# The weights of one stretch split into high and low parts by DMAs instead of by two engines

## The chip, the cores and the metric

The kernel runs on one core of one Trainium2 chip. The metric is the device time of one execution in microseconds. Engine names are those of the profile: PE is the matrix engine (PEld its weight loads), DVE the vector engine, ACT the scalar engine, POOL the general engine, SP the engine that issues most DMAs. Before the change two runs took 1109.42 and 1110.84 us, median 1110.13 us.

## What is computed

One decoder layer over 512 tokens of 2048 features, in float32: an input RMSNorm, one projection with 7728 columns, attention in three branches (NSA, 16 heads), a gated linear recurrence (HGRN2, 8 heads), a norm and a SiLU gate on each group's output, an output projection, the residual and a last norm. Cut to what matters here:

```
h = rmsnorm(x, norm_in[l])
proj = h @ w_in[l]
(q_a, k_cmp, v_cmp, k_slc, v_slc, k_win, v_win, gate_a, z_a,
 q_h, f_h, i_h, z_h) = jnp.split(proj, split_at, axis=-1)
o_a = nsa_mixer(q_a, k_cmp, ...)
o_h = hgrn2_mixer(q_h, f_h, i_h, lbs[l])
o_a = head_rmsnorm(o_a, nsa_out_norm[l], NSA_HEADS) * jax.nn.silu(z_a)
o_h = head_rmsnorm(o_h, hgrn_out_norm[l], HGRN_HEADS) * jax.nn.silu(z_h)
x = x + jnp.concatenate([o_a, o_h], axis=-1) @ w_out[l]
return rmsnorm(x, final_norm)
```

The products of the projections need more precision than one pass of PE's rounded type (float32r) gives. So each operand is written as a sum of a rounded high part and a float32r low part, and each product takes three matmuls: high by high, high by low, low by high.

## The kernel before, in words

**A load.** The weights come in pieces of 512 KB, 1024 columns of 128 partitions (two tiles of 512 columns in `proj_tm`, lines 342 to 344, four tiles of 256 in `proj_fm`, lines 317 to 319). `load_w` (line 269) makes one piece ready: `load_raw` issues its DMA on SP (line 139), ACT rounds it into the high part (the CAST of line 275), DVE subtracts that from the raw piece into the low part (line 276). Then PE runs 24 matmuls of 512 columns on the piece. Raw, high and low each take one of ten buffers of the pool `w` (`WBUF`), so one piece holds three of them until PE, or for the raw one DVE, is done.

**The stretch of the change** begins with `hgrn_v(0)` (the values of four HGRN2 heads) and ends where the output projection begins. It has 72 pieces: 8 of `hgrn_v(0)`; then 44 while the eight heads of `hgrn_head` run between them; then 20 for the gates (`z_proj`) with `gate_chunk` between them. A head is a chain of small steps: DVE scales its keys and queries level by level, POOL copies one piece of queries (line 737), ACT copies others (lines 747, 751, 771, 792, 802, 814), and PE makes the products from them (lines 722, 767, 778, 800, 810, 812).

**What sets the order.** `run` draws pieces of several generators in the ratio of their stated costs. A scheduler then places each engine's instructions; from there each engine goes through its own list strictly in order, and an instruction that waits holds everything behind it on that engine. DMAs are issued in the same way by the engine in whose list they stand.

Of the kernel before, what the change touches and what calls it, by code (L numbers as in the profile page):

```python
# [10 lines left out]
FP32 = mybir.dt.float32  # L11
F32R = mybir.dt.float32r
I32 = mybir.dt.int32
AF = mybir.ActivationFunctionType
ALU = mybir.AluOpType
AX = mybir.AxisListType

P = 128
# [25 lines left out]
def hymba_layer(ctx: ExitStack, tc: tile.TileContext, x, norm_in, w_in, pe_k, w1_k, w2_k,  # L44
# [43 lines left out]
    def run(*gens):  # L88
        """Emits the pieces of several streams, each at the pace of its stated cost."""
        st = [[g, t, 0.0] for g, t in gens]  # L90
        while st:
            e = min(st, key=lambda e: e[2] / e[1])
            try:
                c = next(e[0])
                e[2] = max([o[2] / o[1] for o in st if o is not e]) * e[1] + 1e-6 if c is None else e[2] + c
            except StopIteration:
                st.remove(e)

    def chain(*gens):
        for g in gens:  # L100
            yield from g

    def upto(gen, cost):
        """The stream's next pieces, up to a cost."""
        while cost > 0:
            c = next(gen, None)
            if c is None:
                return
            cost -= c
            yield c  # L110
# [18 lines left out]

# [1 line left out]
    warm = const.tile([1, 1], FP32, name="warm")  # L131
# [9 lines left out]

    # the input by columns: first features and number of tiles of each step, its tiles of tokens, its weights
    FIRST = ((0, 2), (2, 2), (4, 4), (8, 4), (12, 4))
# [24 lines left out]

# [1 line left out]
    hT = [[], []]  # L170
# [29 lines left out]
    def x_norm():  # L200
        """The factor of each token: on the partitions, its half, and along the columns."""
        ss = sm(NT, "ss")
        nc.vector.tensor_reduce(ss, ss_in, AX.X, ALU.add)
        nc.vector.tensor_copy(rs[:, 0, :], rsqrt(ss, NT, 1.0 / D, "rx"))
        nc.vector.tensor_scalar(rs[:, 1, :], rs[:, 0, :], 0.5, None, ALU.mult)
        bp = ps_tp()
        for t in range(NT):
            nc.tensor.transpose(bp[:, t * P:(t + 1) * P], rs[:, 0, t:t + 1].broadcast_to([P, P]), ident)
        nc.scalar.copy(rs_bc, bp)
# [19 lines left out]

# [1 line left out]
    dist = const.tile([P, 512], FP32, name="dist")  # L231
# [27 lines left out]

    # rows that a block of right-hand columns takes, for each level: first row and width within the step  # L260
    for mi, (h, step, lo, width) in enumerate([(1, 2, 0, 1), (2, 4, 0, 2), (4, 8, 2, 2), (4, 8, 0, 2),
# [5 lines left out]

# [1 line left out]
    def load_w(src, k0, kt, c0, c, wt=None, raw=None):  # L269
        if raw is None:  # L270
            raw = load_raw(src, k0, kt, c0, c)
        if wt is None:
            wt = (b4("w", WBUF, F32R), b4("w", WBUF, F32R))
        hi, lo = [w[:, 0:kt * c].rearrange("p (k c) -> p k c", k=kt) for w in wt]
        nc.scalar.copy(hi, raw)  # L275
        nc.vector.tensor_tensor(lo, raw, hi.bitcast(FP32), ALU.subtract)  # L276
        return hi, lo
# [26 lines left out]
    def proj_fm(acc, c0, c):  # L304
        """Columns c0.. of the projection, features on the partitions; accumulators are appended to acc."""
        n = c // P
        kt = min(8, WCOLS // c)
        acc += [pj() for _ in range(n)]
        mm = 0.215 * 3
        for k0 in range(0, NK, kt):  # L310
            hi, lo = load_w(w_in2, k0, kt, c0, c)
            for j in range(n):
                for k in range(kt):
                    kk = k0 + k
                    hh, hl = hT[0][kk], hT[1][kk]
                    wh, wl = hi[:, k, j * P:(j + 1) * P], lo[:, k, j * P:(j + 1) * P]
                    nc.tensor.matmul(acc[j], wh, hh, start=kk == 0, stop=False)  # L317
                    nc.tensor.matmul(acc[j], wh, hl, start=False, stop=False)  # L318
                    nc.tensor.matmul(acc[j], wl, hh, start=False, stop=kk == NK - 1)  # L319
                    if k % 4 == 3 or k == kt - 1:  # L320
                        yield mm * (k % 4 + 1)

    def proj_tm(acc, src, aT, c0, c, done=None):
        """The same with tokens on the partitions: aT is stationary, the weights move."""
        kt = WCOLS // c
        acc += [pj() for _ in range(NT)]
        mm = 0.215 * 3 * c / 512
        groups = [[(k0, min(kt, NK - k0))] for k0 in range(0, NK, kt)]
        if len(groups) > 2:
            groups[-2:] = [groups[-2] + groups[-1]]  # L330
        for gr in groups:
            end = sum(gr[-1])
            while end > len(aT[0]):
                yield None
            ws = [load_w(src, k0, n, c0, c) for k0, n in gr]
            for t in range(NT):
                o = acc[t][:, 0:c]
                for (k0, n), (hi, lo) in zip(gr, ws):
                    for k in range(n):
                        kk = k0 + k  # L340
                        ah, al = aT[0][kk][:, t * P:(t + 1) * P], aT[1][kk][:, t * P:(t + 1) * P]
                        nc.tensor.matmul(o, ah, hi[:, k, :], start=kk == 0, stop=False)  # L342
                        nc.tensor.matmul(o, al, hi[:, k, :], start=False, stop=False)  # L343
                        nc.tensor.matmul(o, ah, lo[:, k, :], start=False, stop=kk == NK - 1)  # L344
                if done is not None and end == NK:
                    done(t, acc[t])
                yield mm * (end - gr[0][0])

# [1 line left out]
    kc_hi = const.tile([P, P], F32R, name="kc_hi")  # L350
# [5 lines left out]
    def blocks(acc, pcol):  # L356
        """Shifted copies of the projected rows, then the blocks with their position terms."""
        kv = []
# [75 lines left out]

# [1 line left out]
    def split_dma(acc_ps, scale, dsts):  # L436
# [12 lines left out]
    def make_kd(g2, b):  # L449
        """Keys of a branch for two groups: the parts hi and lo, each on both halves of the partitions.  # L450
        The keys of the second branch have the compressed ones in front."""
        acc = []
# [52 lines left out]
    def scores(e, i, b):  # L505
        """Scores of a tile of queries and what the softmax makes of them; the sum comes along."""
        h, yv = e["h"], e["yv"]
# [25 lines left out]
    def flip(e, i, b, y):  # L533
        """The weights with the keys on the partitions."""
        n = (i + 1) * P
# [24 lines left out]
    def weigh(e, i):  # L560
        """Values times weights for two tiles of queries, the two branches on two halves of the array."""
        g = e["h"] // 4
# [105 lines left out]

# [1 line left out]
    o_h = [None] * HH  # L670

    def hgrn_head(hh, x0, f, vt):
# [43 lines left out]
        def mm192(x, sections):  # L716
            """Products of the 128 keys of each tile with 192 columns; the masked parts go to dg."""
            for jp in range(2):
# [15 lines left out]

        # the diagonal and level 1
        for jp in range(2):
# [49 lines left out]
        off = lv["off"]  # L786
        # keys with the tokens on the partitions, states at the ends of the tiles
        tps = ps_tp()
# [57 lines left out]

# [1 line left out]
    mT = [[], []]  # L848
# [50 lines left out]

# [1 line left out]
    KC, VC = [], []  # L901
# [10 lines left out]
    fill = [make_q(1), make_q(2), make_kd(1, 0), make_q(3), make_kd(1, 1)] + [make_q(p) for p in range(4, 8)]  # L912
    run((attention(), 160), (chain(*fill, hgrn_qf(0)), 135))
    run((hgrn_v(0), 41))
    sz = [[] for _ in range(4)]
# [7 lines left out]

# [1 line left out]
    ys = [[None] * 4 for _ in range(NT)]  # L925
# [25 lines left out]
    def last_chunk():  # L951
        for t in range(NT):
# [16 lines left out]
            nc.vector.tensor_scalar(pre, pre, 1.0 / D, EPS, ALU.mult, ALU.add)  # L969
            # 1 / sqrt of the mean square: a guess from the bits, then three steps of Newton  # L970
            v, g, u = [a[:, i:i + 1] for i in range(3)]
# [7 lines left out]
            for c in (1, 0, 2, 3):  # L979
# [7 lines left out]
                nc.sync.dma_start(out=out2[t * P:(t + 1) * P, c * 512:(c + 1) * 512], in_=y)  # L987

    last_w = []
    for c in range(3):  # L990
# [39 lines left out]
```

## Time and profile before

| | |
|---|---|
| median of the runs | 1110.13 us |
| span of the profiled execution | 1109.5 us |
| PE busy | 1090.7 us (98%) |
| DVE busy | 579.9 us (52%) |
| ACT busy | 395.7 us (36%) |
| POOL busy | 71.3 us (6%) |
| DMA queue of SP | 108.65 MB, 34.1% of 16 engines |

A span runs from the first to the last instruction of one profiled execution. Busy is the time in which an engine has an instruction in work. Consecutive matmuls overlap, so a busy PE is judged by the start of each matmul against the start of the next. "Idle before" an instruction is put down to what ended it.

### The profile page before, as it was taken

To read this page: it belongs to the slowest core of one execution; us is meant where nothing else is said; L and a number is where in the kernel's file an instruction comes from. 1 tells how busy PE (TensorE), PEld (TensorE's weight loads), DVE (VectorE), ACT (ScalarE), POOL (GpSimd) and SP (SyncE) were. 2 spreads that over 40 slices of the span, in tenths; PEclk is the share of its full clock that TensorE was granted. 3 is DMA by queue.
4 is the path that set the end of the run, shared out by engine and by line. 5 is a ranking of instruction groups with operands and counts; after the bars stand their busy time and mean duration, and the time that the engine had idled before them with its cause. 6 is when DMAs were issued, how large, how long until landed. Compare 5 with 4: busy or idle time off the path is not lost.

```text
span 1109.5 us, 15405 instructions
## 1 busy us (share of the span) xinstructions
PE 1090.7 (98%) x5842; PEld 903.8 (81%) x5842; DVE 579.9 (52%) x1478; ACT 395.7 (36%) x838; POOL 71.3 (6%) x126
## 2 busy tenths in 40 slices
PE   7999999999999999999999999999999999999996
PEld 6899987877777876888888888888888888887886
DVE  4614336676655746316545547546677637324233
ACT  6422326545445544222222322223333323224221
POOL 5002000110200200000000000000000000101000
PEclk9999999999999999999999999999999999999998
DMA  8446463232422211233222322222223333346323
GB/s 260 125 131 190 115 151 97 58 95 58 115 62 73 57 39 39 78 93 96 76 77 57 95 77 77 77 78 75 76 81 90 95 95 115 112 125 208 115 95 124
DMA packets 91753, 109.63 MB, mean 99 GB/s; under 512 B 5584, under 2 KB 60448, under 8 KB 91680
## 3 DMA queue, kind: packets, MB, share of 16 engines
q1 hardware_dynamic: 91680, 108.65, 34.1%
q8 instruction: 46, 0.75, 0.3%
q14 instruction: 27, 0.22, 0.1%
HBM read 93.95 MB, written 4.19 MB: 88 GB/s over the span
## 4 chain that ended last, share of the span: by engine, by line
PE 95%; DMA 2%; DVE 1%; ACT 1%; issue 0%; SPq 0%; ACTq 0%; DVEq 0%
PE pj L342 13%; PE pj L343 13%; PE pj L344 13%; PE pj L317 10%; PE pj L318 10%; PE pj L319 10%; PE ot L571 4%; PE pj L539 3%; PE lp L722 3%; PE lp L514 2%; PE lp L515 2%; PE pj L963 1%; PE pj L962 1%; PE pj L964 1%; PE lp L393 1%; DMA s<-in_x_dram 1%
## 5 line engine op out<-in xcount | busy, mean ns | idle before, releaser
L276 DVE TENSOR_TENSOR w<-w,w 128x1024 fp32r<-128x1024 f32 (+3 forms) x151 | 183.1, 1213 | 238.3 <-PE pj L343 78.5
L275 ACT CAST w<-w 128x1024 fp32r<-128x1024 f32 (+3 forms) x151 | 156.3, 1036 | 290.1 <-DMA w<-in_w_in_dram 191.2
L342 PE MATMUL pj<-w,hh 128*128 128x512 f32 (+2 forms) x608 | 228.8, 377 | 0.0
L343 PE MATMUL pj<-w,hl 128*128 128x512 f32 (+2 forms) x608 | 225.1, 370 | 0.0
L344 PE MATMUL pj<-w,hh 128*128 128x512 f32 (+2 forms) x608 | 224.8, 371 | 0.0
L317 PE MATMUL pj<-hh,w 128*128 128x512 f32 x480 | 195.6, 407 | 0.0
L318 PE MATMUL pj<-hl,w 128*128 128x512 f32 x480 | 189.2, 394 | 0.0
L319 PE MATMUL pj<-hh,w 128*128 128x512 f32 x480 | 188.8, 393 | 0.0
L344 PEld LDWEIGHTS pj<-w,hh 128*128 128x128 f32 x608 | 114.2, 188 | 18.6
L342 PEld LDWEIGHTS pj<-w,hh 128*128 128x128 f32 x608 | 114.5, 188 | 18.1 <-ACT s L479 0.4
L343 PEld LDWEIGHTS pj<-w,hl 128*128 128x128 f32 x608 | 114.5, 188 | 17.9
L319 PEld LDWEIGHTS pj<-hh,w 128*128 128x128 f32 x480 | 90.2, 188 | 19.1 <-issue 0.2
L317 PEld LDWEIGHTS pj<-hh,w 128*128 128x128 f32 x480 | 90.2, 188 | 18.5 <-issue 2.6
L318 PEld LDWEIGHTS pj<-hl,w 128*128 128x128 f32 x480 | 90.3, 188 | 17.4 <-issue 1.5
L529 ACT ACTIVATE s<-s,mn 128x128 f32<-128x128 f32 (+3 forms) x128 | 71.7, 560 | 73.8 <-DVE mn L522 72.0
L522 DVE CUSTOM_DVE_ANT_0 s<-s,lp 128x128 f32<-128x128 f32 (+3 forms) x128 | 60.6, 482 | 34.3 <-PE lp L515 29.9
L539 PE MATMUL pj<-ident,s 128*128 128x128 f32 x320 | 57.0, 277 | 0.9 <-ACT s L556 0.5
L571 PE MATMUL ot<-s,s 128*64 128x256 f32 (+1 forms) x384 | 49.7, 353 | 0.9 <-ACT s L556 0.6
L539 PEld LDWEIGHTS pj<-ident,s 128*128 128x128 f32 x320 | 38.9, 140 | 12.2 <-ACT s L529 3.9
L571 PEld LDWEIGHTS ot<-s,s 128*64 128x64 f32 x384 | 28.0, 136 | 18.8 <-issue 4.6
L558 DVE COPY s<-pj 128x256 f32<-128x256 f32 (+1 forms) x96 | 38.0, 397 | 8.9 <-PE pj L539 8.5
L556 ACT COPY s<-pj 128x128 f32<-128x128 f32 (+1 forms) x96 | 29.4, 308 | 30.4 <-DVE s L558 15.4
(243 smaller groups left out, 1365.4 us busy)
## 6 DMA issues: line engine op xcount, KB each, us to landing
w<-in_w_in_dram SPq DMA_DIRECT2D x115, 512.0 KB, 3.7
w<-in_w_out_dram SPq DMA_DIRECT2D x32, 512.0 KB, 3.8
s<-in_x_dram SPq DMA_DIRECT2D x28, 256.0 KB, 6.0
s<-s SPq DMA_DIRECT2D x56, 128.0 KB, 2.3
out_dram<-s SPq DMA_DIRECT2D x16, 256.0 KB, 2.9
w<-in_w_in_dram SPq DMA_DIRECT2D x5, 456.0 KB, 4.6
w<-in_cmp_w_k_dram SPq DMA_DIRECT2D x4, 512.0 KB, 6.3
w<-in_cmp_w_v_dram SPq DMA_DIRECT2D x4, 512.0 KB, 4.0
```

The costliest lines, as they stand in the source:

```text
L275: nc.scalar.copy(hi, raw)
L276: nc.vector.tensor_tensor(lo, raw, hi.bitcast(FP32), ALU.subtract)
L317: nc.tensor.matmul(acc[j], wh, hh, start=kk == 0, stop=False)
L318: nc.tensor.matmul(acc[j], wh, hl, start=False, stop=False)
L319: nc.tensor.matmul(acc[j], wl, hh, start=False, stop=kk == NK - 1)
L342: nc.tensor.matmul(o, ah, hi[:, k, :], start=kk == 0, stop=False)
L343: nc.tensor.matmul(o, al, hi[:, k, :], start=False, stop=False)
L344: nc.tensor.matmul(o, ah, lo[:, k, :], start=False, stop=kk == NK - 1)
L522: nc.vector.tensor_tensor_reduce(out=y[:, 0:n], in0=e["bias"][:, 384 - i * P:512], in1=lp[:, w:w + n], scale=1.0, scalar=3e38, op0=ALU.add ...
L529: nc.scalar.activation(y[:, 0:n], y[:, 0:n], AF.Exp, bias=mn, scale=-1.0, accum_out=e["ls"][:, 2 * i + b:2 * i + b + 1])
L539: nc.tensor.transpose(tps[:, j * P:(j + 1) * P], y[:, j * P:(j + 1) * P], ident)
L571: nc.tensor.matmul(e["ot"][b * 64:(b + 1) * 64, q0:(i + 1) * P], v_tok[j][:, b * 256 + g * DH:b * 256 + (g + 1) * DH], e["pt"][b][pi][:, o ...
```

## The change

A flag `by_dma` is set before `hgrn_v(0)` and cleared before the output projection's loads. While it is set, `load_w` issues on POOL a DMA that reads the weights as float32 and writes them as float32r into the high part, lets ACT write the negative of the high part into the low part's buffer, and issues on POOL a second DMA that reads the same weights again and adds them to that buffer. No raw buffer is taken and no DVE instruction is issued. The diff without lines that only drop comments:

```diff
+    by_dma = [False]
+
     def load_w(src, k0, kt, c0, c, wt=None, raw=None):
+        if by_dma[0]:
+            hi, lo = [b4("w", WBUF, F32R)[:, 0:kt * c].rearrange("p (k c) -> p k c", k=kt) for _ in range(2)]
+            dram = src[k0 * P:(k0 + kt) * P, c0:c0 + c].rearrange("(k p) c -> p k c", p=P)
+            nc.gpsimd.dma_start(out=hi, in_=dram)
+            nc.scalar.mul(lo, hi.bitcast(FP32), -1.0)
+            nc.gpsimd.dma_start(out=lo, in_=dram, accum_op=ALU.add)
+            return hi, lo
         if raw is None:
             raw = load_raw(src, k0, kt, c0, c)
...
     run((attention(), 160), (chain(*fill, hgrn_qf(0)), 135))
+    by_dma[0] = True
     run((hgrn_v(0), 41))
...
+    by_dma[0] = False
     last_w = []
```

In the changed program 275 is the high part's DMA, 276 the negation on ACT, 277 the low part's DMA; lines of the HGRN2 heads are nine higher than before (737 is 746, 747 is 756, 751 is 760).

POOL's list before, where the last head of the attention ends (line 592) and the first HGRN2 head begins (line 737); a name in brackets is an engine or a DMA counter that the row waits for:

```order
L592 TENSOR_TENSOR s_985_4277<-s_1065_4566 128x4x64 [waits DMAHW0_49,DMAHW7_49,DVE_49,Activation_49]
L592 TENSOR_TENSOR s_985_4277<-s_1094_4688 128x4x64 [waits DVE_49]
L737 COPY s_1043_4481<-s_1142_5038 128x2x64 [waits DVE_49]
L737 COPY s_1044_4482<-s_1142_5038 128x2x64 [waits DMAHW4_49,DVE_49]
L737 COPY s_1045_4485<-s_1190_5352 128x2x64 [waits DMAHW2_49,DVE_49]
```

POOL's list of the changed program at the same place; each load is a high part (L275) and a low part (L277), whose buffer number is one higher:

```order
L277 DMA w_1140_5040<-in_w_in_dram 128x4x256 [waits DMASW2_49,Activation_49]
L277 DMA w_1144_5081<-in_w_in_dram 128x4x256 [waits DMASW3_49,Activation_49]
L275 DMA w_1153_5161<-in_w_in_dram 128x4x256 [waits DMASW4_49,PE_49]
L277 DMA w_1154_5162<-in_w_in_dram 128x4x256 [waits DMASW5_49,PE_49,Activation_49]
L275 DMA w_1157_5216<-in_w_in_dram 128x4x256 [waits DMASW6_49,PE_49]
L746 COPY s_1043_4481<-s_1134_5030 128x2x64 [waits DVE_49]
L746 COPY s_1044_4482<-s_1134_5030 128x2x64 [waits DVE_49]
L275 DMA w_1167_5261<-in_w_in_dram 128x4x256 [waits DMASW7_49,PE_49]
L277 DMA w_1158_5217<-in_w_in_dram 128x4x256 [waits DMASW0_49,Activation_49]
```

Where two copies stood next to each other in POOL's list, 144 DMAs now stand around them. Each low part's DMA waits for ACT. The next load's high part stands behind it in 60 of 72 loads; in 12 loads (7, 10, 13, 29, 30, 53, 61, 62, 65, 69, 70, 71) the high part stands ahead of the low part of the load before it.

ACT's list before, around the first copies of the first HGRN2 head (lines 747 and 751):

```order
L275 CAST w_1169_5229<-w_1168_5227 128x1024 [waits DMAHW5_49,DVE_49]
L747 COPY s_1155_5110<-s_1142_5038 128x2x64 [waits DVE_49]
L747 COPY s_1156_5111<-s_1142_5038 128x2x64
L275 CAST w_1180_5275<-w_1179_5273 128x1024 [waits DMAHW6_49,DVE_49]
L751 COPY s_1155_5110<-s_1142_5038 128x2x64 [waits DVE_49]
```

ACT's list of the changed program at the same place:

```order
L276 ACTIVATE w_1158_5217<-w_1157_5216 128x1024 [waits DMASW6_49,DMASW5_49]
L756 COPY s_1145_5100<-s_1134_5030 128x2x64 [waits DVE_49]
L756 COPY s_1146_5101<-s_1134_5030 128x2x64
L276 ACTIVATE w_1168_5262<-w_1167_5261 128x1024 [waits DMASW7_49]
L760 COPY s_1145_5100<-s_1134_5030 128x2x64 [waits DVE_49]
```

The negations stand where the casts stood, ahead of the same copies; what they wait for is now a DMA of POOL.

## Rows read from the trace of the kernel before

**Rows 1.** Windows of the stretch: start:end, length, busy by engine, granted clock, DMA.
```profile
core 0: us, PE busy (x) PEld busy (x) DVE busy (x) ACT busy (x) POOL busy (x), PEclk, DMA share, GB/s
505.00:806.00 301.00, 300.94 (x1609) 251.61 (x1607) 172.05 (x444) 83.56 (x162) 5.62 (x14) 1.00 0.28 77
806.00:922.00 116.00, 116.00 (x536) 95.83 (x535) 72.44 (x183) 41.32 (x55) 0.00 (x0) 1.00 0.30 87
```

**Rows 2.** Groups by line and form, 455 to 922 us: busy us, mean ns | idle.
```profile
L342 PE MATMUL pj<-w,hh 128*128 128x512 f32 x384 | 153.2, 399 | 0.0
L344 PE MATMUL pj<-w,hh 128*128 128x512 f32 x384 | 150.5, 392 | 0.0
L343 PE MATMUL pj<-w,hl 128*128 128x512 f32 x384 | 150.3, 391 | 0.0
L276 DVE TENSOR_TENSOR w<-w,w 128x1024 fp32r<-128x1024 f32 x72 | 88.1, 1224 | 113.6 <-PE pj L343 51.1 <-PE pj L318 29.8 <-ACT w L275 11.5
L317 PE MATMUL pj<-hh,w 128*128 128x512 f32 x198 | 80.3, 406 | 0.0
L319 PE MATMUL pj<-hh,w 128*128 128x512 f32 x198 | 77.6, 392 | 0.0
L318 PE MATMUL pj<-hl,w 128*128 128x512 f32 x198 | 77.4, 391 | 0.0
L275 ACT CAST w<-w 128x1024 fp32r<-128x1024 f32 x72 | 75.6, 1050 | 161.9 <-DMA w<-in_w_in_dram 134.7 <-DVE s L731 6.5 <-DVE s L728 6.0
```

**Rows 3.** Timeline of PE inside `hgrn_v(0)`: start us, us, engine and line.
```profile
458.83 0.39 PE L342 MATMUL pj<-w,hh 128*128 128x512 f32 x1
459.05 0.39 PE L343 MATMUL pj<-w,hl 128*128 128x512 f32 x1
459.28 0.39 PE L344 MATMUL pj<-w,hh 128*128 128x512 f32 x1
```

**Rows 4.** Windows of line 317 alone: projection matmuls of `proj_fm` between the heads.
```profile
505.00:806.00 301.00, 76.44 (x188) 1.00 0.28 77
```

**Rows 5.** Windows of line 342 alone: first matmuls of `proj_tm` by stage.
```profile
505.00:806.00 301.00, 64.26 (x159) 1.00 0.28 77
806.00:922.00 116.00, 64.03 (x162) 1.00 0.30 87
```

**Rows 6.** Weight DMAs on SP, 455 to 922 us: issue ns min/median/max, time to landing.
```profile
L139 SPq DMA_DIRECT2D w<-in_w_in_dram x68: 367/368/368, 459.0 to 893.1; - x68
...
DMA to landing us min/median/max: 3.5/3.7/5.0
```

**Rows 7.** Window of the start, where the 16 DMA engines are full.
```profile
12.00:20.00 8.00, 8.00 (x46) 6.86 (x45) 5.27 (x7) 8.00 (x24) 3.15 (x11) 1.00 1.06 377
```

**Rows 8.** POOL's copies of the heads, line 737: ns min/median/max.
```profile
L737 POOL COPY s<-s x16: 287/348/1258, 503.3 to 778.4; 128x128 f32<-128x128 f32 x16
```

**Rows 9.** Timeline of ACT in the first head: start us, us, what [idle before].
```profile
506.04 0.51 ACT L747 COPY s<-s 128x128 f32<-128x128 f32 x2
507.42 1.05 ACT L275 CAST w<-w 128x1024 fp32r<-128x1024 f32 x1 [0.87 <-DVE w L276]
509.98 0.50 ACT L751 COPY s<-s 128x128 f32<-128x128 f32 x2 [1.51 <-DVE s L701]
519.76 1.05 ACT L275 CAST w<-w 128x1024 fp32r<-128x1024 f32 x1 [5.23 <-DMA w<-in_w_in_dram]
523.52 0.52 ACT L771 COPY s<-tp 32x128 f32<-32x128 f32 x2 [2.70 <-PE tp L767]
```

## The prediction

> **What bounds the kernel now.** I read the windows first. Over the two later stages of the stretch PE is busy for 300.94 of 301 us and 116.00 of 116 us at a granted clock of 1.00 [rows 1]; no other engine but PE's own weight loads is busy for more than 63% of either. A busy PE could still be a slow one, so the timeline comes next: matmuls of 512 columns start 0.22 to 0.23 us apart [rows 3], so a load's 24 matmuls take 24 x 0.2265 = 5.4 us. The groups by line tell how far PE is from that pace: the plain matmul lasts 390 ns, and what the six lines take beyond it is 384 x (9 + 2 + 1) ns + 198 x (16 + 2 + 1) ns = 8.4 us [rows 2]. That is all that PE loses to late weights or late heads, so 8.4 us is the most that a change to the loads could win here: 0.8% of 1110.
>
> The casts on ACT idle for 134.7 us before a landing and the subtractions on DVE for 51.1 + 29.8 us before a buffer that PE must free [rows 2]. These waits are of engines that run ahead of PE; they cost nothing now. What the reader must take from them is that ACT's queue already stands still for its weights, by up to 5.2 us at one place of the first head [rows 9], and PE does not notice.
>
> **What a load needs in each stage.** Between the heads 188 + 159 groups of three matmuls run [rows 4, 5]; eight make a load, so 44 loads in 301 us: PE asks for one every 6.8 us. In the gates' stage 162 groups are 20 loads in 116 us: one every 5.8 us. The 8 loads of the first stage come every 5.4 us, but their DMAs stand among the last steps of the attention, so five loads (ten buffers, two each) can be ready before PE asks.
>
> **What goes and what replaces it.** Removed: 72 subtractions of 1.22 us on DVE, 88.1 us [rows 2], and 72 SP issues. DVE is busy for 172 of 301 us [rows 1] and PE loses no more than the 8.4 us above, so this is worth between 0 and 8.4 us; I take 0. ACT's cast of 1.05 us [rows 2] becomes a negation of as many elements in the same place; the nearest row is the cast itself, so 0 either way. The buffers carry five loads instead of three: 0, since PE waits for none now.
>
> Added: 144 DMAs on POOL, which had 14 copies to do between the heads. They form a chain. POOL's list is in order, and in 60 of 72 loads it reads high part, low part, high part of the next load. The low part waits for ACT's negation, that for the high part's landing. So the next high part isn't even issued until this one has landed and been negated, where SP used to issue its raw loads ahead. The length of one turn of the chain:
>
> - POOL issues the low part. No DMA of POOL is in the trace. SP's issue of the same shape takes 0.37 us [rows 6]; a POOL instruction takes 0.29 to 1.26 us [rows 8]. I take the upper end, 1.26, since POOL is the engine that does it and a DMA of 256 or 512 rows is its largest instruction here; the ends are 0.37 and, doubled for want of a row, 2.5.
> - The low part's transfer, which the next high part's packets queue behind. With the DMA engines full, 377 GB/s flow [rows 7], so 512 KB take 1.39 us. An accumulating DMA reads both the weights and the buffer: between 1.39 and 2.8 us; I take the middle, 2.1. It hides the issue of the next high part.
> - The high part's transfer: 1.39 us at the same rate; twice that if rounding on the way halves the rate (2.8, the far end).
> - The rest of a landing. Issue to landing has a median of 3.7 us [rows 6]; less 0.37 of issue and 1.39 of transfer this leaves 1.94 us.
> - The negation, 1.05 us [rows 2].
>
> Together 1.26 + 2.1 + 1.39 + 1.94 + 1.05 = 7.7 us. In the 12 loads whose high part stands ahead, landing and negation overlap the load before, and only the transfers count: 2.1 + 1.39 = 3.5 us.
>
> The Trainium skill (DMA: Bandwidth & Descriptors, Specifications) gives about 1 us to the first byte for a DMA that POOL issues, against 0.6 us for SP; with 1.0 us in place of 1.26 the turn would be 7.5 us and the sum below 14 us less. No run here shows it yet.
>
> **The sum by stages.** Heads: 40 turns of 7.7 and 4 of 3.5 are 322 us against 301: +21. Gates: 13 turns and 7 short ones are 125 us against 116: +9. First stage: 7 turns and a short one are 57 us against 43, but the five loads made ahead cover it: 0.
>
> Then what queues behind the negations. ACT's copies for the heads alternate with them in its list, as they do with the casts now [rows 9], as POOL's copies stand behind its DMAs, and PE's matmuls of the head wait for both. A negation now waits for its landing: up to 2.1 + 1.39 + 1.94 = 5.4 us. Each head passes five or six negations; the price lies between 0 (copies always early) and 5.4 us at each of five. Before, such a wait of 5.2 us passed without loss, so most are covered; where the weights run late, that cover is thinner. I take one full wait for each head: 8 x 5.4 = 43 us.
>
> 21 + 9 + 43 = +73 us. The profiled span is 1109.5 us and the median of the runs 1110.1, 0.6 us around it; 1109.5 + 0.6 + 73 = 1183 us. What is late next is not the matmuls of a load but the head's products, lines 731 and 819 of the new text.
>
> A rule speaks for more. What the trace bears out is only one read per load: 77 GB/s at a share of 0.28 [rows 1]. The Trainium skill (Collectives: The Full Stack, The bandwidth ceiling: the fold count and why AG ≠ RS ≠ AR) says that a DMA that adds is slower because it has two sources to read, which halved the rate. By that rule the low part takes the far end, 2.8 us, the turn 8.4 us, and the sum 52 + 23 + 8 x 6.1 = 124 us, 1234 us in all. The range holds it.
>
> **The rivals.**
>
> *The chain keeps up (not slower).* POOL issues as fast as SP and the added read costs nothing: 0.37 + 1.39 + 1.39 + 1.94 + 1.05 = 6.1 us a turn. The place is POOL's list between two high parts; the point is 7.2 us, where 40 turns and 4 short ones just fill 301 us. For it: ACT's long waits cost nothing today, and there are five loads of buffers. Against: POOL's own rows, and two transfers where there was one. The gates' stage then fits as well, 13 x 6.1 + 7 x 2.8 = 99 of 116 us. Time: 1110 less up to 8 us, plus up to 7 at a head or two: 1102 to 1117. Chance 0.15.
>
> *Transfers at half rate.* Rounding and adding on the way slow the DMA engines: 2.8 us for the high part, 4.2 for the low one. The turn is 1.26 + 4.2 + 2.8 + 1.94 + 1.05 = 11.25 us, the short one 7.0. Heads 478 us (+177), gates 195 us (+79): +256 us, 1366 us; the copies are then hidden in the chain. Against: the engines have 70% of their time free [rows 1]. For: no row shows either kind of transfer. Chance 0.18, from 1270 up to 1400.
>
> *Faster.* DVE's 88 us were holding PE after all, beyond the 8.4 us that the matmuls show. Nothing in the rows speaks for it. Below 1088: chance 0.02.
>
> **How the numbers follow.** The forecast has 0.65, and its own ends are 1120 (issue 0.7 us, few head waits) and 1270 (added read in full, longer issue). The predicted time is 1183. The range 1112 to 1310 leaves out the faster half of the first rival (0.07), the upper part of the second (0.11) and the last one (0.02). A measurement of this kernel tells 2% from no change, 22 us. Slower by more: all of the forecast but 0.04, and the half-rate case, 0.79; within 2%: the first rival and that 0.04, 0.19; faster 0.02.
>
> **What would show it.** Right: PE's busy share between the heads falls from 100% towards 90%; PE's idle time there ends with ACT's or POOL's copies, the lines 756, 760 and 746; negations on ACT wait for the high part's DMA for much more than 134.7 us in all; high parts follow each other on POOL every 7 to 8 us. If they follow every 6 us and PE stays full, the first rival holds. If the DMA share passes 0.8 in the gates' stage, the second does. I am wrong if POOL issues a DMA in well under 0.7 us, if a converting DMA takes several times a copy's time, or if the heads' copies turn out to run far ahead of PE.

## The result, and the profile after

Two runs of the changed kernel took 1241.89 and 1243.20 us, median 1242.55: 1.119 times the time before, 95% interval [1.116, 1.122], or 132 us more. The profiled execution has a span of 1240.2 us at a mean granted clock of 0.955. The change is slower, as forecast, and inside the range; the forecast's +73 us is little more than half of the measured +132.

Windows of the same two stages (between the first and last product of the heads, then the gates), in the columns of [rows 1]:

```profile
511.00:915.00 404.00, 333.81 (x1607) 274.94 (x1607) 123.36 (x401) 82.59 (x162) 92.85 (x103) 0.89 0.61 117
915.00:1053.00 138.00, 121.54 (x537) 99.11 (x537) 53.18 (x166) 40.97 (x56) 31.19 (x32) 0.94 0.65 138
```

The same 1,600 matmuls that filled 301 us [rows 1] now lie in 404 us: +103. The gates' stage grew from 116 to 138 us: +22. The rest, 6 us, is what the stage of `hgrn_v(0)` leaves over: its first matmul starts at 456.51 us (458.83 before), 2.3 us sooner, and the heads' first product at 510.7 (505.1 before), so the stage itself is 7.9 us longer; 5.3 us of that is one wait of PE for POOL's first copy of line 746. PE stands idle for 70 of the 404 us, and its busy time went up by 33 us although its work is the same. The granted clock of 0.89 tells most of why: it wasn't full all the time.

Groups by line and form, 455 to 1060 us, the columns of [rows 2] (three to four of the 72 loads were made before 455 us, so the counts are 68 and 69):

```profile
L277 POOL DMA_DIRECT2D w<-in_w_in_dram x69 | 84.6, 1226 | 400.2 <-ACT w L276 251.9 <-ACT s L756 47.6 <-ACT s L811 32.2
L275 POOL DMA_DIRECT2D w<-in_w_in_dram x68 | 74.8, 1115 | 43.1 <-PE pj L352 26.8 <-PE pj L353 14.4 <-PE pj L328 1.9
L276 ACT ACTIVATE w<-w 128x1024 fp32r<-128x1024 f32 x69 | 73.1, 1059 | 377.4 <-DMA w<-in_w_in_dram 364.8 <-issue 12.6
L731 PE MATMUL lp<-s,s 128*128 128x192 f32 x192 | 44.8, 386 | 45.0 <-ACT s L760 24.0 <-POOL s L746 9.1 <-DVE s L715 7.6
L328 PE MATMUL pj<-hh,w 128*128 128x512 f32 x195 | 79.2, 406 | 1.1 <-DMA w<-in_w_in_dram 1.1
```

Read these as a ring. POOL waits for ACT (252 us and more), ACT waits for a DMA (365 us; the casts waited 134.7 us [rows 2]), and the DMA is POOL's own, issued after the last wait. For a free buffer, that is for PE, POOL waits only 43 us. The profile puts the rest of POOL's 400 us down to copies that ACT ran right behind a negation (L756, L811); the DMA waits for the negation. PE's waits end at the heads' copies, hardly at weights (1.1 us). One turn of the ring is seen in POOL's timeline (start us, us, what, idle before and its end), with ACT's negation of the middle load below it:

```profile
540.12 1.29 POOL L277 DMA_DIRECT2D w<-in_w_in_dram  x1 [8.22 <-ACT s L780]
540.87 1.32 POOL L275 DMA_DIRECT2D w<-in_w_in_dram  x1
549.45 1.27 POOL L277 DMA_DIRECT2D w<-in_w_in_dram  x1 [7.26 <-ACT w L276]
550.21 1.25 POOL L275 DMA_DIRECT2D w<-in_w_in_dram  x1
558.01 1.19 POOL L277 DMA_DIRECT2D w<-in_w_in_dram  x1 [6.55 <-ACT s L811]
```

```profile
548.10 1.06 ACT L276 ACTIVATE w<-w 128x1024 fp32r<-128x1024 f32 x1 [8.17 <-DMA w<-in_w_in_dram]
```

Low part, 0.75 us later the next high part, then 7 to 8 us of nothing. A turn takes 9.3 us and 8.6 us here, and 404 us for 44 loads make 9.2 us a load. Landings of the two kinds, high part (line 275) first; each group ends with its landing time:

```profile
L275 POOL DMA_DIRECT2D w<-in_w_in_dram x72: 721/1208/1462, 415.2 to 1026.6; - x72
...
DMA to landing us min/median/max: 3.8/6.8/9.2
```

```profile
L277 POOL DMA_DIRECT2D w<-in_w_in_dram x72: 1182/1202/1345, 420.7 to 1035.1; - x72
...
DMA to landing us min/median/max: 5.5/5.8/9.5
```

A high part's issue takes 0.72 us at the least but 1.21 in the median, and it lands 6.8 us after its issue where SP's raw load took 3.7 [rows 6].

### The profile page after: what moved, and what is told of

Read it like the earlier page. It is cut to its first block, busy times and chain, and to the rows that moved or that the text cites. A ratio compares the mean times of both kernels' runs of the same rounds, so it can differ in the third digit from the quotient of the medians.

```text
span 1240.2 us, 15436 instructions
## 1 busy us (share of the span) xinstructions
PE 1127.7 (91%) x5842; PEld 930.1 (75%) x5842; DVE 498.7 (40%) x1406; ACT 393.6 (32%) x838; POOL 212.9 (17%) x270
## 4 chain that ended last, share of the span: by engine, by line
PE 50%; issue 32%; POOL 8%; DMA 6%; DVE 2%; ACT 2%; SPq 0%; POOLq 0%; ACTq 0%; DVEq 0%
PE pj L352 6%; PE pj L353 6%; PE pj L351 6%; PE pj L326 5%; PE pj L327 5%; DMA w<-in_w_in_dram 5%; PE pj L328 5%; POOL w L275 4%; POOL w L277 3%; PE ot L580 3%; PE pj L548 2%; PE lp L523 2%; PE lp L524 1%; PE pj L974 1%; PE pj L973 1%
## 5 line engine op out<-in xcount | busy, mean ns | idle before, releaser
L351 PE MATMUL pj<-w,hh 128*128 128x512 f32 (+2 forms) x608 | 234.2, 385 | 1.6 <-DVE s L904 1.6
L353 PE MATMUL pj<-w,hh 128*128 128x512 f32 (+2 forms) x608 | 231.3, 381 | 0.8 <-DMA w<-in_w_in_dram 0.8
L326 PE MATMUL pj<-hh,w 128*128 128x512 f32 x480 | 199.1, 415 | 0.0
L276 ACT ACTIVATE w<-w 128x1024 fp32r<-128x1024 f32 x72 | 76.2, 1059 | 379.9 <-DMA w<-in_w_in_dram 367.3
L328 PE MATMUL pj<-hh,w 128*128 128x512 f32 x480 | 191.7, 399 | 1.1 <-DMA w<-in_w_in_dram 1.1
L277 POOL DMA_DIRECT2D w<-in_w_in_dram x72 | 88.2, 1225 | 410.7 <-ACT w L276 262.3
L285 DVE TENSOR_TENSOR w<-w,w 128x1024 fp32r<-128x1024 f32 (+3 forms) x79 | 95.3, 1206 | 122.2 <-ACT w L284 61.4
L351 PEld LDWEIGHTS pj<-w,hh 128*128 128x128 f32 x608 | 118.2, 194 | 21.0 <-DVE s L904 2.0
L353 PEld LDWEIGHTS pj<-w,hh 128*128 128x128 f32 x608 | 117.7, 194 | 21.1 <-DMA w<-in_w_in_dram 1.4
L284 ACT CAST w<-w 128x1024 fp32r<-128x1024 f32 (+3 forms) x79 | 80.7, 1022 | 125.1 <-DMA w<-in_w_in_dram 54.0
L275 POOL DMA_DIRECT2D w<-in_w_in_dram x72 | 77.9, 1097 | 61.1 <-PE pj L352 26.8
L731 PE MATMUL lp<-s,s 128*128 128x192 f32 x192 | 44.8, 386 | 45.0 <-ACT s L760 24.0
L710 DVE TENSOR_TENSOR s<-s,s 128x256 f32<-128x256 f32 x56 | 23.8, 424 | 151.9 <-POOL s L746 73.3
L731 PEld LDWEIGHTS lp<-s,s 128*128 128x128 f32 x192 | 38.5, 225 | 50.9 <-ACT s L760 31.2
```

Of the source, the lines that this page charges most:

```text
L275: nc.gpsimd.dma_start(out=hi, in_=dram)
L276: nc.scalar.mul(lo, hi.bitcast(FP32), -1.0)
L277: nc.gpsimd.dma_start(out=lo, in_=dram, accum_op=ALU.add)
L731: nc.tensor.matmul(lp[:, j * 192:(j + 1) * 192], k[:, jj * P:(jj + 1) * P], x[jp][:, j, :], start=True, stop=True)
```

## The experiments

**High parts ahead.** Every load is made as in the changed kernel, with the same instructions, but the high part's DMA of the next load is issued ahead of this one's negation and low part, throughout. `specs` lists the 72 loads in order.

```diff
...
-            nc.gpsimd.dma_start(out=hi, in_=dram)
+            while len(ready) <= 1 and specs:
+                k0_, kt_, c0_, c_ = specs.pop(0)
...
+                nc.gpsimd.dma_start(out=h, in_=d)
+                ready.append(((k0_, kt_, c0_, c_), h, l, d))
+            spec, hi, lo, dram = ready.pop(0)
...
             nc.scalar.mul(lo, hi.bitcast(FP32), -1.0)
             nc.gpsimd.dma_start(out=lo, in_=dram, accum_op=ALU.add)
```

> The same loads, DMAs and negations; only the order on POOL differs: the high part of a later load is issued ahead of the low part of this one throughout, not in 12 of 72 loads. Theory (the chain): the turn of 9 to 10 us (issue of the low part, the high part's landing of 6.8 us, negation of 1.06 us) is what costs, so with landings overlapped most of the 132 us goes: 1110 to 1145 us, and PE is busy over 97% between the heads. Rival (transfers): the converting and adding DMAs hold the 16 engines too long; 144 of them stay, so the time stays above 1200 us and the DMA share goes on at 0.6 with PE idle.

Measured: 1109.57 us over ten runs, 0.9995 of before, interval [0.9985, 1.0005]. All 132 us are gone. Two of its windows:

```profile
500.00:600.00 100.00, 100.00 (x518) 84.13 (x517) 38.05 (x127) 27.55 (x51) 33.37 (x38) 1.00 0.87 163
700.00:800.00 100.00, 99.91 (x544) 83.19 (x542) 44.72 (x146) 28.66 (x57) 28.21 (x35) 1.00 0.74 147
```

POOL's timeline, lines 283 (high part) and 288 (low part), and the high parts' landing:

```profile
535.50 0.71 POOL L283 DMA_DIRECT2D w<-in_w_in_dram  x1 [4.30 <-PE pj L339]
536.42 1.20 POOL L288 DMA_DIRECT2D w<-in_w_in_dram  x1 [0.21 <-issue]
537.17 0.99 POOL L757 COPY s<-s 128x128 f32<-128x128 f32 x2
542.56 0.73 POOL L283 DMA_DIRECT2D w<-in_w_in_dram  x1 [4.40 <-PE pj L339]
```

```profile
L283 POOL DMA_DIRECT2D w<-in_w_in_dram x72: 712/732/1694, 416.5 to 886.9; - x72
...
DMA to landing us min/median/max: 3.7/4.0/9.5
```

POOL now waits for PE, as DVE's subtractions did before [rows 2]: a load every 7 us here, which is PE's pace. The DMA engines carry 0.74 to 0.87 of their time without harm, so neither their rate nor the two DMAs of a load are the loss; the order in POOL's list is. That the high part now lands 4.0 us after its issue, against 6.8 behind a low part, gives the size of what it queued behind: 2.8 us, of which 0.5 is POOL's own longer issue (1.21 us against 0.73).

**The second DMA without the add.** The same program, but the second DMA only converts and overwrites the negative, so the low part doesn't hold the remainder.

```diff
-            nc.gpsimd.dma_start(out=lo, in_=dram, accum_op=ALU.add)
+            nc.gpsimd.dma_start(out=lo, in_=dram)
```

> The changed kernel with the second DMA a plain converting copy: it doesn't add, so the low part holds the rounded weights and not the remainder. Orders, waits and number of DMAs are the same. Theory (the chain, with the added read as a part of the turn): the next high part queues behind a transfer that is 1.4 us rather than some 3 us long, so the turn falls from 9.3 to about 7.7 us and the time to 1140 to 1175 us. Rival (the turn is latency and issue; the added read hides beside them): 1225 to 1245 us.

Measured: 1141.67 us, one run. The rows of the second DMA and of the first DMA's landing:

```profile
L277 POOL DMA_DIRECT2D w<-in_w_in_dram x72: 713/716/749, 421.3 to 931.0; - x72
...
DMA to landing us min/median/max: 3.7/3.9/5.6
```

```profile
L275 POOL DMA_DIRECT2D w<-in_w_in_dram x72: 696/721/942, 415.8 to 924.1; - x72
...
DMA to landing us min/median/max: 3.8/4.7/6.3
```

The add makes the issue 1.20 us long instead of 0.72 and the landing 5.8 us instead of 3.9. In the order of the changed kernel it costs 101 of the 132 us; the chain without it still turns in 7.3 us between the heads (the median distance of second DMAs on POOL), over PE's 6.8. From the first second DMA to the last, POOL needs 509.7 us (421.3 to 931.0) against 614.4 in the changed kernel (420.7 to 1035.1): 104.7 us less, where the kernel lost 100.9.

**The negation on POOL.**

```diff
-            nc.scalar.mul(lo, hi.bitcast(FP32), -1.0)
+            nc.gpsimd.tensor_scalar(lo, hi.bitcast(FP32), -1.0, None, ALU.mult)
```

> The negation moves from ACT to POOL, between its two DMAs; ACT's list holds no weights in the stretch, so the heads' copies on ACT wait for no landing. The turn on POOL stays, longer by what POOL needs more than ACT for 1024 elements. Theory (the chain): loads come no faster, so PE still waits, now for weights: 1215 to 1290 us. Rival (only what queues behind the negations on ACT costs; the weights themselves are early): 1110 to 1170 us.

Measured: 1365.45 us, one run, over every expectation, since the negation takes far longer on POOL:

```profile
L276 POOL TENSOR_SCALAR w<-w 128x1024 fp32r<-128x1024 f32 x72 | 199.8, 2775 | 356.8 <-DMA w<-in_w_in_dram 315.3 <-issue 11.7 <-PE pj L353 11.6
```

Its size is a second test of the ring. A turn became 2.775 - 1.06 = 1.715 us longer, and the median of the long turns between the heads (those whose high part is issued behind a low part) went from 9.23 to 10.94 us. 72 such additions make 123.5 us; the kernel took 122.9 us more than the changed one. An agreement that close is partly luck: the short turns grew by more, from 3.2 to 6.8 us in mean, and two long waits of POOL for a buffer went away. But the ring as a whole, from POOL's first low part to its last, grew by 119.0 us; what lengthens it reaches the end in full:

```profile
L277 POOL DMA_DIRECT2D w<-in_w_in_dram x72: 1243/1250/1442, 423.9 to 1157.2; - x72
```

The mean granted clock fell from 0.955 to 0.916 in this run and left an extra of at most 4 us, 122.9 less 119.0. PE waited for weights only in part, 66.2 us at line 353 and 10.3 at 328; for the rest it waited for POOL's copies of the heads, which now stand behind the negations on POOL:

```profile
PE lp L731 <- POOL s L746: 125.1, 8, 25.0
PE pj L353 <- DMA w<-in_w_in_dram: 66.2, 14, 10.2
```

**The heads' copies of POOL on DVE.**

```diff
-            nc.gpsimd.tensor_copy(x0[jp][:, :, P:192].unsqueeze(3), right2(qp, jp, 1))
+            nc.vector.tensor_copy(x0[jp][:, :, P:192].unsqueeze(3), right2(qp, jp, 1))
```

> The heads' copies on POOL go to DVE, so POOL has only DMAs; the chain is as before. Theory (the chain, with what queues behind it on ACT and POOL): PE's waits for POOL's copies, some 9 us, and DVE's of 73 us behind them shrink, but the chain sets the pace: 1220 to 1243 us. Rival (the heads' copies behind POOL's waiting DMAs are the main loss): under 1190 us.

Measured: 1241.85 us, one run: no change, as the theory of the chain has it.

**All copies of the heads on DVE**, those of ACT too:

```diff
-                nc.scalar.copy(x[jp][:, :, 64:128].rearrange("p j (b h) -> p j b h", h=2 * h), right2(qp, jp, 2 * h))
+                nc.vector.tensor_copy(x[jp][:, :, 64:128].rearrange("p j (b h) -> p j b h", h=2 * h), right2(qp, jp, 2 * h))
...
-        nc.scalar.copy(o, op)
+        nc.vector.tensor_copy(o, op)
```

> All copies of the heads' products that ACT (new lines 756, 760, 780, 801, 811, 823) and POOL (746) made go to DVE, which no load touches in the changed kernel; ACT's list between the heads then holds little but the negations. If the prediction's 43 us are a cost of their own (copies held behind negations, on top of the chain's pace), most of it comes back: 1190 to 1215 us, and PE no longer waits for the heads. If the chain of POOL sets the pace and the copies are only the place where PE meets it, little changes: 1225 to 1255 us, a high part still every 9 us or so between the heads, and PE's idle time moves from the copies to the weights (lines 326 and 351 after a DMA).

Measured: 1235.05 us, one run; 7.5 us came back. The time is the ring's: its 44 low parts between the heads go out within 390 us, against 397 in the changed kernel. The place was not the one expected. PE's waits between the heads (engine, line, waited for: us, times, longest):

```profile
PE lp L731 <- DVE s L761: 27.7, 2, 21.2
PE tp L776 <- DVE s L715: 24.1, 2, 20.7
PE lp L731 <- DVE s L746: 19.1, 1, 19.1
...
PE pj L353 <- DMA w<-in_w_in_dram: 1.7, 1, 1.7
```

PE still doesn't wait for weights but for DVE, seldom and long. ACT's timeline and DVE's around one of these waits show what DVE waited for:

```profile
566.21 1.06 ACT L276 ACTIVATE w<-w 128x1024 fp32r<-128x1024 f32 x1 [8.11 <-DMA w<-in_w_in_dram]
575.11 1.06 ACT L276 ACTIVATE w<-w 128x1024 fp32r<-128x1024 f32 x1 [7.84 <-DMA w<-in_w_in_dram]
584.06 1.06 ACT L276 ACTIVATE w<-w 128x1024 fp32r<-128x1024 f32 x1 [7.90 <-DMA w<-in_w_in_dram]
585.03 0.61 ACT L853 ACTIVATE s<-s 128x512 f32<-128x512 f32 x1
```

```profile
558.26 0.69 DVE L852 TENSOR_TENSOR s<-pj,rs_bc 128x512 f32<-128x512 f32 x1 [1.40 <-PE pj L328]
585.67 0.74 DVE L683 TENSOR_SCALAR s<-s,lbt 128x512 f32<-128x512 f32 x1 [26.72 <-ACT s L853]
```

The tanh of line 853, a step in preparing a head, has its input from 559 us on and stands behind three negations until 585. ACT's whole list moves at the ring's pace, and whatever of a head is on it brings that pace to PE.

**One half alone.** First the high part by DMA, with the raw load on SP and the subtraction on DVE:

```diff
+            raw = load_raw(src, k0, kt, c0, c)
             nc.gpsimd.dma_start(out=hi, in_=dram)
-            nc.scalar.mul(lo, hi.bitcast(FP32), -1.0)
-            nc.gpsimd.dma_start(out=lo, in_=dram, accum_op=ALU.add)
+            nc.vector.tensor_tensor(lo, raw, hi.bitcast(FP32), ALU.subtract)
```

> Half of the change: the high part by the converting DMA on POOL; a raw copy of the weights by SP as before, and DVE subtracts. ACT has no part in a load any more; POOL's DMAs wait for buffers alone. Theory (the chain): no DMA of POOL waits for a landing, so nothing is lost: 1103 to 1120 us. Rival (a converting DMA is slow in itself, or POOL's issues are): still over 1150 us. Rival (ACT's casts were holding PE before): under 1100 us.

Then the low part by DMA, with the raw load on SP and the cast on ACT:

```diff
+            raw = load_raw(src, k0, kt, c0, c)
-            nc.gpsimd.dma_start(out=hi, in_=dram)
+            nc.scalar.copy(hi, raw)
             nc.scalar.mul(lo, hi.bitcast(FP32), -1.0)
             nc.gpsimd.dma_start(out=lo, in_=dram, accum_op=ALU.add)
```

> The other half: raw weights by SP and the cast on ACT as before, then the negation on ACT and the adding DMA on POOL. ACT does two instructions of 1.05 us a load; POOL's low parts wait for ACT, but no landing stands behind them on POOL. Theory (the chain): the landings on SP run ahead again, so little is lost, only what the heads' copies wait behind on POOL, and three buffers a load again: 1110 to 1150 us. Rival (the adding DMA is what costs, by its own 5.8 us to landing): over 1180 us.

Measured, four runs each: 1129.43 us, 1.0171 of before [1.0152, 1.0189], above what was expected, and 1116.45 us, 1.0056 [1.0039, 1.0074]. The second one has every adding DMA and the negation and loses 6 us: the price of the adds lies in what queues behind them. The first one shows another ring, now through DVE:

```profile
POOL w L276 <- DVE w L277: 280.4, 48, 8.5
DVE w L277 <- DMA w<-in_w_in_dram: 90.7, 24, 6.1
ACT s L760 <- DVE s L710: 79.8, 15, 13.1
```

POOL's high part waits for a buffer that DVE's subtraction of an earlier load must free, that subtraction waits for a landing, and ACT's copies of the heads wait for DVE. That this is where its 19 us went is read from these rows; no run tried it by itself, and PE's own waits in this run sum to only 13.7 us. Its mean granted clock is 0.990, against 0.997 before; how the 19 us divide stays open.

**The gates alone.** The flag is set only behind the heads, for what the expectation counts as the last 20 loads.

```diff
-    by_dma[0] = True
     run((hgrn_v(0), 41))
...
+    by_dma[0] = True
     run((fill, 41), (gate_chunk(0, o_nsa[0:4], 2, sz[0]), 10.5))
```

> The change in the last 20 of the 72 loads alone (the gates, after the heads). Theory (a turn of 9.3 us against a need of 5.8 us a load, 7 of 20 with landings overlapped): the loss of this stage in the changed kernel, some 22 us, stays and the 109 us of the earlier stages go: 1120 to 1140 us. Rival (the loss comes through the heads' copies alone): 1108 to 1114 us.

Measured: 1139.04 us over four runs, 1.0248 [1.0231, 1.0266]. The trace has 38 DMAs of POOL, so the flag caught 19 loads, not 20:

```profile
w<-in_w_in_dram POOLq DMA_DIRECT2D x38, 512.0 KB, 6.3
```

That is 28 us for 19 loads, against 22 us for the stage inside the full change; why it is more here, no run tells. The loss goes with the loads; the stage has no heads.

## Why the prediction came out as it did

**PE bounds, nothing to win: right.** With the ring broken (high parts ahead), two DMAs a load take 0.9995 of the time before; the 72 subtractions taken off DVE won nothing.

**The chain on POOL: right in kind, and its turn too short, 7.7 us for 9.2.** Term by term:

- Issue of the low part: 1.26 us put in, and the issue does take 1.20, but the next high part is issued after 0.75 us, so the term on the chain is 0.75 (-0.5).
- The low part's transfer: 2.1 put in, the middle between one read and two. The high part lands 6.8 us after its issue behind it and 4.0 without it, so 2.8 (+0.7), 0.5 of it in POOL's longer issue. An estimate by another way comes near: the adding DMA lands in 5.8 us and the plain one in 3.9, and 0.49 of the difference is issue, so 1.4 us on top of the 1.39 of one read.
- The high part's own transfer and landing: 1.39 + 1.94 = 3.33 put in, on the ground that its issue was hidden. 4.0 measured, POOL's 0.72 us of issue with it (+0.7).
- Negation: 1.05 for 1.06.
- Hand-overs between the queues: not in the sum. 9.2 - 0.75 - 2.8 - 4.0 - 1.06 = 0.6 us. By the timelines of POOL and ACT, 0.1 us of it lies between landing and negation and 0.3 between the negation's end and the low part (548.10 + 1.06 to 549.45 above); the other 0.2 is that the high parts of the long turns between the heads land in 7.0 us, not 6.8. ACT's copies for the heads hardly hold the ring.

The rule on the second read that the prediction weighed (the Trainium skill, Collectives: The Full Stack, The bandwidth ceiling: the fold count and why AG ≠ RS ≠ AR) is borne out in direction, not to the factor of two. The page says it of the adding step of a ReduceScatter. Here the two halves of the change compare 72 DMAs of either kind. The row of POOL's DMA queue (packets, MB, share of the span of 16 engines) in the run with the high part alone, then with the low part alone:

```profile
q0 software_dynamic: 25728, 37.75, 13.3%
q0 software_dynamic: 25728, 37.75, 22.0%
```

Over spans of 1129.5 and 1114.5 us, the adding DMAs hold the engines 1.63 times as long as the converting ones; SP's raw loads ran beside them in both. The rule's end of the forecast, 1234 us, lay nearest the 1242.6 measured, but by luck: 48.8 us of its +124 is the copy term that doesn't exist as such (next point but one), and without it the sum is +75. The same skill's longer start of a POOL DMA (DMA: Bandwidth & Descriptors, Specifications; 1 us against 0.6) agrees roughly with the whole way to landing: 4.0 us against SP's 3.7 [rows 6].

**The stages.** Heads: 44 loads of 9.2 us are 404 us; +21 put in, +103 measured, the step that failed in size. By POOL's timeline the low parts of these 44 loads go out within 397 us. The 40 long turns take 9.6 us in mean, not 7.7, which is 77 of the missing 82 us. Two of them last 15 us because POOL waits there for a buffer that PE must free (most of the 26.8 us at L275 above); the other 38 take 9.3. The four short turns, put in at 3.5 us, took 1.4, 1.4, 3.9 and 6.1, 3.2 in mean. PE left the stage 7 us further behind POOL's list than it entered it, which is the rest. Gates: +9 put in, +22 measured. The 13 long turns took 9.4 us and the seven short ones 4.2, 152 us in all; 14 of that was covered, since POOL's list was 32 us ahead of PE when the stage began and 18 when it ended. First stage: 0 put in, 6 measured; the five loads made ahead did cover the weights, but not POOL's first copy for the heads.

**The heads' copies behind negations: 43 us put in, and no such term.** They are the place at which PE loses its time, and not far off in size: between the heads PE waits 24.0 us at line 731 after line 760, as forecast, then 14.8 at line 787, 11.4 at 821 and 1.1 at 809, 51 us for ACT's copies in all (line 819, which the prediction names, isn't among them). But this is not a cost beside the chain's. PE's 70 us of waiting and its 33 us of longer work are together the 103 us by which the stage grew, and the ring's 44 turns by themselves are 96 us longer than PE's need (397 us against 301). Moving all the copies off ACT and POOL gave 7.5 us back, though it left other steps of a head, such as the tanh, on ACT. The prediction counted the delay twice, once as pace and once as waits, and the 43 us made up for part of the 101 us that the chain's own terms were short of: the right total was nearer than its parts, by luck.

**The clock: not in the prediction.** Before, it was 1.00 throughout both stages [rows 1]. After, windows of two pieces show the lower of the two levels, 1.2 GHz:

```profile
535.50:545.80 10.30, 5.82 (x19) 4.74 (x20) 1.84 (x5) 1.46 (x3) 2.08 (x2) 0.50 0.58 104
590.10:600.40 10.30, 7.04 (x23) 5.12 (x22) 1.43 (x5) 1.46 (x3) 1.93 (x2) 0.50 0.67 153
```

PE's timeline at the second one:

```profile
589.20 0.45 PE L776 MATMUL tp<-s,s 128*32 128x32 f32 x16 [3.17 <-DVE s L715]
...
594.42 1.12 PE L787 MATMUL tp<-s,s 128*64 128x64 f32 x8 [3.26 <-ACT s L780]
...
597.34 0.63 PE L353 MATMUL pj<-w,hh 128*128 128x512 f32 x1
597.77 0.63 PE L351 MATMUL pj<-w,hh 128*128 128x512 f32 x1
```

Matmuls start 0.43 us apart, against 0.2265 [rows 3]. PE had stood idle for 3.2 us just before, behind line 715, and stands again within the piece. Between the heads there are 14 such stretches, 86 us in all, in which PE is busy for 62 us; half of that, 31 us, is nearly all of the 33 us by which PE's busy time grew. It looks like a consequence that costs little more: PE would have waited in that time for the ring, and the run with the negation on POOL lost hardly more than its ring grew (122.9 us against 119.0) at a still lower clock. No run held the clock up while the ring stood, so how much of the 132 us it owns by itself stays open.

**The rivals.** Transfers at half rate in both DMAs falls: the converting one is as fast as a plain one, and the DMA share stayed at 0.61 and 0.65 in the two stages. A high share, the sign named for this rival, would not have proved it: the run with the high parts ahead has 0.87 in a window between the heads and loses nothing. That the chain keeps up is what the reordered kernel does, not this one. What was to show the forecast right did: PE below 90%, ACT's landing waits up from 134.7 to 365 us. High parts came every 9 us, not every 7 to 8.

## What to carry to other kernels

When a queue that issues in order carries a DMA that waits for another engine, and that engine waits for a DMA of the same queue, the queue's lookahead is one: work out the turn, and issue the next independent transfer ahead of the waiting one. The same instructions in the other order were worth 133 us here. And when a ring sets the pace, the waits it causes elsewhere are the same time seen again; a sum has the turn or the waits in it, not both.

## What the runs showed beside

- A converting DMA (float32 to float32r, 512 KB) costs no more transfer than a plain one: 4.0 us to landing, 3.7 on SP. POOL's issue of it takes 0.71 to 0.73 us, SP's 0.37.
- An adding DMA takes 1.20 us of POOL's time, and a converting one issued right behind it 1.21 us instead of 0.72. The adding one holds the DMA engines 1.63 times as long as a converting one of the same size.
- POOL multiplies 128x1024 elements in 2.78 us, ACT in 1.06.
